# A threshold search with one number per row as its state, VectorE's keys in PSUM, and a one-hot made by one comparison

## The chip, the cores and the metric

One core of one Trainium2 chip runs the whole program in one launch. The metric is the device time in microseconds, median of the runs. The engines are TensorE (PE in the profile, PEld for its weight loads), VectorE (DVE), ScalarE (ACT), GpSimd (POOL) and SyncE (SP), which issues most DMA. SBUF is the on-chip memory, PSUM the accumulator memory that TensorE writes and that VectorE and ScalarE can read and write.

## The reference, cut to what matters

A layer takes 1024 tokens of width 1024 through a token mixer (gated DeltaNet and pooling) and then through a mixture of experts in which each of 16 experts chooses its 128 tokens:

```python
def expert_choice_ffn(h, w_router, w_gate, w_up, w_down):
    B_, L, D = h.shape
    cap = EC_CAPACITY * L // N_EXPERTS                       # 128
    aff = jax.nn.softmax((h @ w_router).astype(jnp.float32), axis=-1)
    top_aff, top_idx = lax.top_k(jnp.swapaxes(aff, 1, 2), cap)
    xe = jax.vmap(lambda hb, ib: hb[ib])(h, top_idx)
    hid = jax.nn.silu(jnp.einsum('becd,edf->becf', xe, w_gate)) * jnp.einsum('becd,edf->becf', xe, w_up)
    ye = jnp.einsum('becf,efd->becd', hid, w_down) * top_aff[..., None].astype(h.dtype)
    combine = lambda ib, yb: jnp.zeros((L, D), yb.dtype).at[ib.reshape(-1)].add(yb.reshape(-1, D))
    return jax.vmap(combine)(top_idx, ye)
```

The output is the final RMS-normalised stream of 1024 x 1024 numbers.

## The kernel before

The work runs in stages. After the token mixer comes the stage of its output projection and the router: it goes over 8 tiles of 128 tokens, and for each one multiplies by `w_out` (matmuls at L1256, into `y`), adds the residual, normalises, transposes and multiplies by the router's weights; `softmax` leaves the affinities in `aff`, 128 tokens x 8 tiles x 16 experts. The first tile of this stage is preceded by the constants of the later search, written by GpSimd (L1362 to L1393), and by `o_norm`, whose power at L1080 (`ro`) also runs on GpSimd; VectorE scales `oa` with it at L1082, and TensorE transposes that at L1105. Every engine executes its instructions in program order.

Then the search finds, for each of 16 experts, the affinity of its 128th best token. `aff` is transposed (L1534) so that each of 128 rows holds 128 affinities of one expert and one token tile; eight rows belong to one expert. The bits of an affinity are split into a high key (`khi`) and a low key (`klo`), and two searches of 7 and 8 rounds find the threshold, two bits in each round. A round compares all keys with three candidates: two on VectorE (L1562, `cmp`) and one on ScalarE with Sign (L1560), each with a sum along the row into `cnt`. A matmul with `same` (L1566) adds up the eight rows of an expert over a first matmul that puts the limits `lim` there (L1565), and VectorE counts from the totals how many candidates hold (L1579, `ge`, sum into `d`). The state of the search is the three candidates `nxt` and the last step `d`; two small instructions (L1568, L1569) make the next candidates and a third (L1558) the offset `c2` for ScalarE. During the first eight rounds ScalarE also rounds halves of the first four weight slices (L1574) and GpSimd subtracts (L1516, `flo`), and before that GpSimd finishes the FFN's input of the last two tiles (L1339, L1340) and stores it to `h2d`.

After the search, scans (L1602, L1603) give each chosen token its place, a transpose brings the places to token order (`tpp`, then `posT`), and `onehot(e)` compares them with the numbers 1 to 128: for expert 0 in one instruction on `tpp`, for the others in eight instructions, one for each token tile. `select` multiplies the one-hot with token numbers and affinities, and `gather` fetches the rows from `h2d` with an indirect DMA by GpSimd.

The expert stage goes over 16 experts with three weight matrices of 8 slices each (512 KB a slice). Each slice is loaded by SyncE's queue into one of 34 buffers, split into two parts (`fhi` on ScalarE, `flo` on VectorE at L1516) and used in six matmuls (L1638). A buffer is loaded again when its split is done. Results are added to `accd` by an indirect DMA (L1744). A last stage normalises and stores.

Of the kernel before, what the change touches and what calls it, by code (L numbers as in the profile page):

```python
# [19 lines left out]
L = 1024  # L20
NT = 8
# [5 lines left out]
CAP = 128  # L27
# [25 lines left out]
def trunk_kernel(ctx, tc, x, c, ctxt, c_ctx, w_mod, b_mod, norm1, norm2, w_in, conv_w, a_log, dt_bias,  # L53
# [154 lines left out]
    pos = [0]  # L208
# [1106 lines left out]
    def softmax(t):  # L1315
# [46 lines left out]
    SEARCH = [(65536.0, i) for i in range(7)] + [(1.0, i) for i in range(8)]  # L1362
    base3 = ES.tile([128, 3], F32, name="base3")
    sgn3 = ES.tile([128, 3], F32, name="sgn3")
    dlt3 = ES.tile([128, len(SEARCH), 3], F32, name="dlt3")
    stp3 = ES.tile([128, len(SEARCH), 3], F32, name="stp3")
    nxt0 = ES.tile([128, 2, 3], F32, name="nxt0")
    lim = ES.tile([128, 3], F32, name="lim")
    for j, v in enumerate((1.0, 2.0, -3.0)):
        POOL.memset(base3[:, j:j + 1], v)  # L1370
        POOL.memset(sgn3[:, j:j + 1], v / abs(v))
        POOL.memset(lim[:, j:j + 1], 0.5 - CAP if j < 2 else L - 2.0 * (CAP - 0.5))
    for n, (unit, i) in enumerate(SEARCH):
        POOL.memset(stp3[:, n, :], unit * 4.0 ** i)
        POOL.tensor_scalar(dlt3[:, n, :], base3, unit * ((4.0 ** (i - 1) if i else 0.0) - 4.0 ** i), None, op0=OP.mult)
    for n, (unit, i, first) in enumerate(((65536.0, 6, 0.0), (1.0, 7, 1.0))):
        POOL.tensor_scalar(nxt0[:, n, :], base3, unit * 4.0 ** i, None, op0=OP.mult)
        for j, v in enumerate((first, first, 0.5 * unit - first)):
            POOL.tensor_scalar(nxt0[:, n, j:j + 1], nxt0[:, n, j:j + 1], v, None, op0=OP.add)
# [12 lines left out]
    slotb = WS.tile([128, 128], BF16, name="slotb")  # L1392
    POOL.tensor_copy(slotb, slots)  # L1393
# [142 lines left out]
    khi = RT.tile([128, 128], F32, name="khi")  # L1536
    klo = RT.tile([128, 128], F32, name="klo")
    cmp = RT.tile([128, 2, 128], F32, name="cmp")
    ki = RT.tile([128, 128], I32, name="ki")
    DVE.tensor_scalar(ki, tpa.bitcast(I32), 0x7fff0000, None, op0=OP.bitwise_and)  # L1540
    DVE.tensor_copy(khi, ki)

    sgn = RT.tile([128, 128], F32, name="sgn")
    zero = RT.tile([128, 1], F32, name="zero")
    DVE.memset(zero, 0.0)
    thr = RT.tile([128, 2], F32, name="thr")

    def search(key, dst, nxt, unit, n):
# [3 lines left out]

        d = zero
        for i in range(n - 1, -1, -1):
            row = SEARCH.index((unit, i))
# [21 lines left out]
            ge = RT.tile([128, 3], F32, name="ge")  # L1577
            d = RT.tile([128, 1], F32, name="d", bufs=2)
# [3 lines left out]
    search(khi, thr[:, 0:1], nxt0[:, 0, :], 65536.0, 7)  # L1582
    ki = RT.tile([128, 128], I32, name="ki")
# [5 lines left out]
    search(klo, thr[:, 1:2], nxt0[:, 1, :], 1.0, 8)  # L1589
# [195 lines left out]
    pos = {}  # L1785
# [65 lines left out]
```

## Time and profile before

| | |
|---|---|
| median of 3 runs | 1363.76 us (1360.57 to 1364.97) |
| profiled execution, time | 1365.92 us |
| profiled execution, span | 1364.2 us |
| TensorE busy | 1261.2 us (92%) |
| VectorE busy | 1029.5 us (75%) |
| ScalarE busy | 751.1 us (55%) |
| GpSimd busy | 390.6 us (29%) |
| DMA, over the span | 241 GB/s |

The span goes from the first to the last instruction of the profiled execution; its time also holds what lies around them. Busy shares are means over stages with different limits, so a stage is read from its own stretch of the span. The granted clock of TensorE is given as a share of 2.4 GHz, and has the levels 1.00 and 0.50.

### The profile page before, as it was taken

The page shows a single profiled execution, that of the slowest core. Times are in us where ns is not written, and L with a number is a line of the kernel's source. Part 1 is how long each engine was busy: PE and PEld are TensorE (multiplying, and loading weights), DVE is VectorE, ACT ScalarE, POOL GpSimd, SP SyncE. Part 2 cuts the span into 40 slices and gives each one's busy share as a digit, 9 for nine tenths or more (in the row PEclk, how much of TensorE's full clock was granted, in tenths as well). Part 3 has the DMA queues.
Part 4 walks back from the last instruction along what each step waited for, and adds up shares of the span by engine and source line. Part 5 has one row for each costly group of instructions (what it writes and reads, how often), then busy time and mean ns, then how long its engine had stood idle before and what let it go on. Part 6 is the DMA issues. An engine that isn't in the chain of part 4 may idle for free.

```text
span 1364.2 us, 26631 instructions
## 1 busy us (share of the span) xinstructions
PE 1261.2 (92%) x10355; PEld 1003.4 (74%) x10355; DVE 1029.5 (75%) x1773; ACT 751.1 (55%) x1103; POOL 390.6 (29%) x394
## 2 busy tenths in 40 slices
PE   5899889989999989989982799999999999999997
PEld 3476777666767779978872688888888888888884
DVE  4763665675775436864659699999999999999995
ACT  5443434343433324333233477777777777777783
POOL 5700552494865113761116000000000000000002
PEclk9999989998999989999995799999999999999999
DMA  9667213212123268634686599999999999999806
GB/s 353 209 193 276 70 37 91 86 49 79 49 79 95 87 221 317 214 128 154 231 322 232 188 340 369 386 385 384 379 383 382 388 381 385 383 382 383 298 4 259
DMA packets 140760, 328.39 MB, mean 241 GB/s; under 512 B 13517, under 2 KB 53082, under 8 KB 140634
## 3 DMA queue, kind: packets, MB, share of 16 engines
q1 hardware_dynamic: 134826, 305.72, 60.8%
q0 software_dynamic: 5376, 19.40, 5.6%
q8 instruction: 81, 1.33, 0.4%
q10 hardware_dynamic: 432, 1.57, 0.3%
q14 instruction: 45, 0.37, 0.1%
HBM read 287.32 MB, written 39.32 MB: 239 GB/s over the span
## 4 chain that ended last, share of the span: by engine, by line
PE 75%; DVE 11%; issue 4%; POOL 4%; DMA 3%; ACT 2%; SPq 0%; POOLq 0%; ACTq 0%; DVEq 0%
PE pg L1638 14%; PE pu L1638 13%; PE pd L1638 12%; PE px L484 11%; PE y L1256 6%; PE sc L923 5%; PE iv L687 2%; DVE acc L428 2%; PE tp L1674 2%; PE gv L132 1%; DMA wm<-in_w_mod_dram 1%; DVE pT L666 1%; DMA Vd<-rows 1%; PE pc L484 1%; DVE T L704 1%
## 5 line engine op out<-in xcount | busy, mean ns | idle before, releaser
L484 PE MATMUL px<-hx,whi 128*128 128x512 f32 x640 | 222.0, 427 | 4.6 <-ACT hx L290 2.7
L1516 DVE TENSOR_TENSOR flo<-rawb,fhi 128x1024 fp32r<-128x1024 f32 x176 | 208.6, 1224 | 11.2 <-ACT fhi L1515 10.5
L1515 ACT ACTIVATE fhi<-rawb 128x1024 fp32r<-128x1024 f32 x176 | 186.1, 1062 | 53.6 <-PE pg L1638 19.0
L1516 DVE TENSOR_TENSOR flo<-rawa,fhi 128x1024 fp32r<-128x1024 f32 x158 | 187.3, 1224 | 12.9 <-ACT fhi L1515 12.2
L1515 ACT ACTIVATE fhi<-rawa 128x1024 fp32r<-128x1024 f32 x158 | 167.2, 1062 | 51.3 <-PE pg L1638 21.9
L1638 PE MATMUL pg<-fhi,lhs 128*128 128x512 f32 x544 | 157.9, 402 | 0.0
L1638 PE MATMUL pu<-fhi,lhs 128*128 128x512 f32 x512 | 146.6, 398 | 0.0
L484 PEld LDWEIGHTS px<-hx,whi 128*128 128x128 f32 x640 | 113.2, 193 | 40.5 <-issue 12.4
L1744 POOL DMA_INDIRECT accd<-ye,ix x15 | 34.6, 2310 | 366.2 <-DVE ye L1742 366.2
L1638 PE MATMUL pd<-fhi,lhs 128*128 128x512 f32 x480 | 134.2, 396 | 0.0
L484 PE MATMUL px<-hx,wlo 128*128 128x512 f32 x320 | 128.5, 402 | 0.0
L1638 PEld LDWEIGHTS pg<-fhi,lhs 128*128 128x128 f32 x544 | 100.8, 190 | 22.6 <-ACT lhs L1676 0.4
L1638 PEld LDWEIGHTS pu<-fhi,lhs 128*128 128x128 f32 x512 | 95.1, 188 | 21.8
L1638 PEld LDWEIGHTS pd<-fhi,lhs 128*128 128x128 f32 x480 | 90.1, 188 | 21.6
L1638 PE MATMUL pg<-flo,lhs 128*128 128x512 f32 x272 | 86.2, 398 | 0.0
L1638 PE MATMUL pu<-flo,lhs 128*128 128x512 f32 x256 | 80.5, 395 | 0.0
L1256 PE MATMUL y<-ohi,mx 128*128 128x512 f32 x256 | 76.4, 404 | 0.8 <-DVE oa L981 0.8
L201 POOL TENSOR_TENSOR wlo<-wraw,whi 128x1024 fp32r<-128x1024 f32 x16 | 41.1, 2568 | 125.2 <-ACT whi L200 125.2
L1638 PE MATMUL pd<-flo,lhs 128*128 128x512 f32 x240 | 75.5, 396 | 0.0
L484 PEld LDWEIGHTS px<-hx,wlo 128*128 128x128 f32 x320 | 61.6, 193 | 14.0
L428 DVE SCALAR_TENSOR_TENSOR acc<-pad,prmT,acc 128x1024 f32<-128x1024 f32 x36 | 66.3, 1843 | 3.6 <-ACT acc L424 3.3
L1664 POOL DMA_INDIRECT xe<-h2d,ix x16 | 16.4, 1027 | 168.7 <-PE pg L1638 120.7
(453 smaller groups left out, 2405.1 us busy)
## 6 DMA issues: line engine op xcount, KB each, us to landing
rawb<-in_w_down_dram SPq DMA_DIRECT2D x61, 512.0 KB, 6.1
rawb<-in_w_gate_dram SPq DMA_DIRECT2D x58, 512.0 KB, 5.1
rawb<-in_w_up_dram SPq DMA_DIRECT2D x57, 512.0 KB, 6.0
rawa<-in_w_gate_dram SPq DMA_DIRECT2D x56, 512.0 KB, 5.0
rawa<-in_w_up_dram SPq DMA_DIRECT2D x54, 512.0 KB, 6.1
rawa<-in_w_down_dram SPq DMA_DIRECT2D x52, 512.0 KB, 6.1
wm<-in_w_mod_dram SPq DMA_DIRECT2D x48, 512.0 KB, 5.7
wraw<-in_w_in_dram SPq DMA_DIRECT2D x20, 512.0 KB, 4.1
```

The lines of the kernel that those rows point to most:

```text
L201: (POOL if pos[0] > 4 else DVE).tensor_tensor(lo[:, :, :n], raw[:, :, :n], hi[:, :, :n].bitcast(F32), op=OP.subtract)
L428: DVE.scalar_tensor_tensor(acc, pad[:, j:j + L], convw(j, ct), acc, op0=OP.mult, op1=OP.add)
L484: PE.matmul(dst, wp[:, k, :], src[hp][:, k, o], start=start and i == 0, stop=stop and i == len(parts) - 1)
L687: PE.matmul(iv[r, u, o:64], pa[r, u, :], PV[r, u, o:64], start=True, stop=True)
L923: PE.matmul(p[:, h, :], lhs(h), rhs(h), start=True, stop=True)
L1256: PE.matmul(ys[t, hf][:, hf, :], l_[:, k, :], r_[:, 512 * hf:512 * hf + 512], start=(k == KORD[0] and i == 0), stop=(k == KORD[-1] and i = ...
L1515: ACT.activation(hi, raw, AF.Copy)
L1516: (eng or DVE).tensor_tensor(lo, raw, hi.bitcast(F32), op=OP.subtract)
L1638: PE.matmul(ps[:, hf, :], l_[:, k, :], r_[:, 512 * hf:512 * hf + 512], start=(k == 0 and n == 0), stop=(k == KD - 1 and n == 2))
L1664: POOL.indirect_dma_start(out=xe[e], out_offset=None, in_=h2d[:, :], in_offset=bass.IndirectOffsetOnAxis(ap=ix[:, 0:1], axis=0))
L1674: PE.transpose(tp[:, q, :], src[:, 128 * k:128 * k + 128], ident)
L1744: POOL.indirect_dma_start(out=accd[:, :], out_offset=bass.IndirectOffsetOnAxis(ap=idx.pop(e)[:, 0:1], axis=0), in_=ye, in_offset=None, com ...
```

## The change

The search's state becomes one number per row, the sum `v`, which `ge` accumulates straight into the constants' column of the next round: `stp5[:, row + 1, 3:4]`, beside a column of constants, which the two additional columns of `lim5` let pass. The candidates are `v` plus constants, so the instructions that made `c2` and `nxt` go. VectorE's keys lie in PSUM, and ScalarE has its own copy in SBUF (`keys`); the mask of integer bits `ki` is in PSUM too. The last tile's softmax leaves its exponentials in PSUM. `onehot` makes its mask by one comparison for every expert. The constants are made by other instructions on GpSimd.

```diff
@@ softmax
-        ACT.activation(a, a, AF.Exp, bias=mxn, accum_out=sm_)
+        ex = logits if t == ORDER[-1] else a
+        ACT.activation(ex, a, AF.Exp, bias=mxn, accum_out=sm_)
         DVE.reciprocal(rc, sm_)
-        DVE.tensor_scalar(a, a, rc, None, op0=OP.mult)
+        DVE.tensor_scalar(a, ex, rc, None, op0=OP.mult)
@@ constants
-    for j, v in enumerate((1.0, 2.0, -3.0)):
-        POOL.memset(base3[:, j:j + 1], v)
-        POOL.memset(sgn3[:, j:j + 1], v / abs(v))
-        POOL.memset(lim[:, j:j + 1], 0.5 - CAP if j < 2 else L - 2.0 * (CAP - 0.5))
+    SEARCH = [(65536.0, i) for i in range(6, -1, -1)] + [(1.0, i) for i in range(7, -1, -1)]
+    cst3 = ES.tile([128, len(SEARCH), 2], F32, name="cst3")
+    stp5 = ES.tile([128, len(SEARCH) + 1, 5], F32, name="stp5")
+    lim5 = ES.tile([128, 5], F32, name="lim5")
+    for j, v in enumerate((0.5 - CAP, 0.5 - CAP, L - 2.0 * (CAP - 0.5), 1.0, 1.0)):
+        POOL.memset(lim5[:, j:j + 1], v)
     for n, (unit, i) in enumerate(SEARCH):
-        POOL.memset(stp3[:, n, :], unit * 4.0 ** i)
-        POOL.tensor_scalar(dlt3[:, n, :], base3, unit * ((4.0 ** (i - 1) if i else 0.0) - 4.0 ** i), None, op0=OP.mult)
-    for n, (unit, i, first) in enumerate(((65536.0, 6, 0.0), (1.0, 7, 1.0))):
-        POOL.tensor_scalar(nxt0[:, n, :], base3, unit * 4.0 ** i, None, op0=OP.mult)
-        for j, v in enumerate((first, first, 0.5 * unit - first)):
-            POOL.tensor_scalar(nxt0[:, n, j:j + 1], nxt0[:, n, j:j + 1], v, None, op0=OP.add)
+        step = unit * 4.0 ** i
+        third = 3.0 * step - 0.5 * unit
+        for j in range(2):
+            POOL.memset(cst3[:, n, j:j + 1], (j + 1) * step - third)
+        POOL.memset(stp5[:, n, 0:3], -step)
+        if n in (0, 7):
+            POOL.memset(stp5[:, n, 3:4], -third - (1.0 if n else 0.0))
+        POOL.memset(stp5[:, n, 4:5], third - (0.75 * step - 0.5 * unit if i else 0.0))
...
-    slotb = WS.tile([128, 128], BF16, name="slotb")
-    POOL.tensor_copy(slotb, slots)
@@ search
-    khi = RT.tile([128, 128], F32, name="khi")
-    klo = RT.tile([128, 128], F32, name="klo")
+    khi = PSR.tile([128, 128], F32, name="khi")
+    klo = PSR.tile([128, 128], F32, name="klo")
+    keys = RT.tile([128, 2, 128], F32, name="keys")
-    ki = RT.tile([128, 128], I32, name="ki")
+    ki = PSR.tile([128, 128], I32, name="ki")
     DVE.tensor_scalar(ki, tpa.bitcast(I32), 0x7fff0000, None, op0=OP.bitwise_and)
+    DVE.tensor_copy(keys[:, 0, :], ki)
     DVE.tensor_copy(khi, ki)
...
+        for row in rows:
+            v = stp5[:, row, 3:4]
             cnt = RT.tile([128, 3], BF16, name="cnt", bufs=8)
-            c2 = RT.tile([128, 1], F32, name="c2", bufs=15)
-            DVE.tensor_tensor(c2, nxt[:, 2:3], d, op=OP.subtract)
-                ACT.activation(sgn, key, AF.Sign, bias=c2, accum_out=cnt[:, 2:3])
+                ACT.activation(sgn, skey, AF.Sign, bias=v, accum_out=cnt[:, 2:3])
             for j in range(2):
-                DVE.scalar_tensor_tensor(cmp[:, j, :], key, d, nxt[:, j:j + 1].to_broadcast([128, 128]),
-                                         op0=OP.subtract, op1=OP.is_ge, accum_out=cnt[:, j:j + 1])
-            tot = PSR.tile([128, 3], F32, name="tot", bufs=2)
-            PE.matmul(tot, ident, lim, start=True, stop=False)
-            PE.matmul(tot, same, cnt, start=False, stop=True)
-            new = RT.tile([128, 3], F32, name="nxt", bufs=8)
-            DVE.scalar_tensor_tensor(new, sgn3, d, nxt, op0=OP.mult, op1=OP.add)
-            DVE.tensor_tensor(new, new, dlt3[:, row, :], op=OP.add)
-            nxt = new
+                DVE.scalar_tensor_tensor(cmp[:, j, :], key, v, cst3[:, row, j:j + 1].to_broadcast([128, 128]),
+                                         op0=OP.add, op1=OP.is_ge, accum_out=cnt[:, j:j + 1])
+            tot = PSR.tile([128, 5], F32, name="tot", bufs=2)
+            PE.matmul(tot, ident, lim5, start=True, stop=False)
+            PE.matmul(tot[:, 0:3], same, cnt, start=False, stop=True)
...
-            DVE.scalar_tensor_tensor(ge, tot, 0.0, stp3[:, row, :], op0=OP.is_ge, op1=OP.mult, accum_out=d)
-        DVE.tensor_tensor(dst, nxt[:, 0:1], d, op=OP.add)
+            DVE.scalar_tensor_tensor(ge, tot, 0.0, stp5[:, row, :], op0=OP.is_ge, op1=OP.mult,
+                                     accum_out=dst if row == rows[-1] else stp5[:, row + 1, 3:4])
+        DVE.tensor_scalar(dst, dst, -1.0, None, op0=OP.mult)
@@ between the searches
+    kl = RT.tile([128, 128], F32, name="kl")
     DVE.tensor_scalar(ki, tpa.bitcast(I32), 0xffff, None, op0=OP.bitwise_and)
-    DVE.tensor_scalar(klo, ki, 1.0, None, op0=OP.add)
-    DVE.scalar_tensor_tensor(klo, khi, thr[:, 0:1], klo, op0=OP.is_equal, op1=OP.mult)
+    DVE.tensor_scalar(kl, ki, 1.0, None, op0=OP.add)
+    DVE.scalar_tensor_tensor(kl, khi, thr[:, 0:1], kl, op0=OP.is_equal, op1=OP.mult)
     DVE.tensor_scalar(khi, khi, thr[:, 0:1], 1.0e6, op0=OP.is_gt, op1=OP.mult)
-    DVE.tensor_tensor(klo, klo, khi, op=OP.add)
+    DVE.tensor_tensor(keys[:, 1, :], khi, kl, op=OP.add)
+    DVE.tensor_tensor(klo, khi, kl, op=OP.add)
@@ onehot
-        if pos is not None:
-            DVE.tensor_tensor(oh, slots[:, None, :].to_broadcast([128, NT, 128]),
-                              pos[:, :, e:e + 1].to_broadcast([128, NT, 128]), op=OP.is_equal)
-        else:
-            for t in range(NT):
-                DVE.tensor_scalar(oh[:, t, :], slotb, posT[:, t, e:e + 1], None, op0=OP.is_equal)
+        DVE.tensor_tensor(oh, slots[:, None, :].to_broadcast([128, NT, 128]),
+                          (posT if pos is None else pos)[:, :, e:e + 1].to_broadcast([128, NT, 128]), op=OP.is_equal)
```

## Rows read from the trace of the kernel before

**Rows 1.** Windows of four stages: stretch, its length, busy times, clock, DMA share, GB/s.

```profile
600.00:620.00 20.00, 16.12 (x76) 13.36 (x75) 7.27 (x14) 5.00 (x9) 8.65 (x36) 0.83 0.51 187
...
660.00:680.00 20.00, 20.00 (x128) 15.99 (x127) 12.07 (x22) 6.40 (x15) 3.62 (x6) 1.00 0.63 216
...
740.00:760.00 20.00, 6.79 (x42) 5.65 (x42) 16.10 (x92) 3.94 (x16) 3.43 (x2) 0.50 0.13 36
...
840.00:1240.00 400.00, 400.00 (x1884) 323.73 (x1883) 386.29 (x470) 315.79 (x326) 36.72 (x22) 1.00 1.02 384
```

**Rows 2.** Timeline, 594 to 612 us: start, duration, engine, line, operation, shapes [idle before].

```profile
594.43 0.10 POOL L1370 MEMSET base<- 128x1 f32 x1
...
594.46 0.10 POOL L1371 MEMSET sgn<- 128x1 f32 x1
...
600.95 0.16 DVE L1079 SCALAR_TENSOR_TENSOR ro<-ro,ssqh 128x4 f32<-128x4 f32 x1
...
604.53 0.14 POOL L1384 IOTA jt<- 128x8 f32 x1
...
606.06 1.05 POOL L1080 TENSOR_TENSOR ro<-ro,mhalf 128x4 f32<-128x4 f32 x1
...
607.89 1.12 PE L1105 MATMUL tp<-ident,oa 128*128 128x128 f32 x4 [3.88 <-DVE oa L1082]
```

**Rows 3.** Timeline around the start of the search, 713 to 722 us.

```profile
714.06 1.36 DVE L1328 TENSOR_SCALAR aff<-aff,sm 128x16 f32<-128x16 f32 x1
...
716.05 0.29 DVE L1540 TENSOR_SCALAR ki<-tp 128x128 int32<-128x128 int32 x1 [0.63 <-PE tp L1534]
...
716.37 1.52 DVE L1541 CAST khi<-ki 128x128 f32<-128x128 int32 x1
...
718.01 0.34 DVE L1562 SCALAR_TENSOR_TENSOR cmp<-khi,zero,nxt 128x128 f32<-128x128 f32 x1
...
721.22 2.35 POOL L1340 TENSOR_TENSOR h<-h,s2b 128x1024 f32<-128x1024 f32 x1
...
721.28 0.15 DVE L1579 SCALAR_TENSOR_TENSOR ge<-tot,stp 128x3 f32<-128x3 f32 x1
...
721.48 2.11 DVE L1558 TENSOR_TENSOR c<-nxt,d 128x1 f32<-128x1 f32 x1
```

**Rows 4.** Timeline of one round of the second search, 744 to 746 us.

```profile
744.54 0.16 DVE L1579 SCALAR_TENSOR_TENSOR ge<-tot,stp 128x3 f32<-128x3 f32 x1
...
744.74 0.16 DVE L1558 TENSOR_TENSOR c<-nxt,d 128x1 f32<-128x1 f32 x1
...
744.82 0.34 DVE L1562 SCALAR_TENSOR_TENSOR cmp<-klo,d,nxt 128x128 f32<-128x128 f32 x1
...
745.02 0.40 ACT L1560 ACTIVATE sgn<-klo,c 128x128 f32<-128x128 f32 x1 [0.73 <-PE tot L1565]
...
745.36 0.09 DVE L1562 DVE_READ_ACCUMULATOR cmp<-klo,d,nxt 128x1 bf16 x1
...
745.57 0.17 PE L1566 MATMUL tot<-cnt,same 128*128 128x3 bf16 x1 [0.64 <-ACT sgn L1560]
...
745.77 0.16 DVE L1579 SCALAR_TENSOR_TENSOR ge<-tot,stp 128x3 f32<-128x3 f32 x1
```

**Rows 5.** Timeline, weight splits on GpSimd, then the way to the first expert.

```profile
728.29 4.64 POOL L1516 TENSOR_TENSOR flo<-rawa,fhi 128x1024 fp32r<-128x1024 f32 x2
...
751.74 0.42 DVE L1602 TENSOR_TENSOR_SCAN cmp<-onesr,ar 128x128 f32<-128x128 f32 x1
...
756.34 1.39 DVE L1621 TENSOR_SCALAR oh<-slotb,posT 128x128 bf16<-128x128 bf16 x8
...
761.58 1.76 PE L1674 MATMUL tp<-ident,xe 128*128 128x128 f32 x7 [3.60 <-DMA xe<-h2d,ix]
```

**Rows 6.** The page's costliest groups: busy, mean ns | idle before, its releaser.

```profile
L1516 DVE TENSOR_TENSOR flo<-rawb,fhi 128x1024 fp32r<-128x1024 f32 x176 | 208.6, 1224 | 11.2 <-ACT fhi L1515 10.5
...
L1744 POOL DMA_INDIRECT accd<-ye,ix x15 | 34.6, 2310 | 366.2 <-DVE ye L1742 366.2
```

More of the change, by code (lines that the diff above doesn't have):

```diff
@@ L1358, in trunk_kernel @@
     DVE.tensor_tensor(prev, d16, same, op=OP.mult)
[L1362 to L1368, printed above, removed]
-    for j, v in enumerate((1.0, 2.0, -3.0)):
-        POOL.memset(base3[:, j:j + 1], v)
-        POOL.memset(sgn3[:, j:j + 1], v / abs(v))
-        POOL.memset(lim[:, j:j + 1], 0.5 - CAP if j < 2 else L - 2.0 * (CAP - 0.5))
-    for n, (unit, i) in enumerate(SEARCH):
-        POOL.memset(stp3[:, n, :], unit * 4.0 ** i)
-        POOL.tensor_scalar(dlt3[:, n, :], base3, unit * ((4.0 ** (i - 1) if i else 0.0) - 4.0 ** i), None, op0=OP.mult)
-    for n, (unit, i, first) in enumerate(((65536.0, 6, 0.0), (1.0, 7, 1.0))):
-        POOL.tensor_scalar(nxt0[:, n, :], base3, unit * 4.0 ** i, None, op0=OP.mult)
-        for j, v in enumerate((first, first, 0.5 * unit - first)):
-            POOL.tensor_scalar(nxt0[:, n, j:j + 1], nxt0[:, n, j:j + 1], v, None, op0=OP.add)
+    SEARCH = [(65536.0, i) for i in range(6, -1, -1)] + [(1.0, i) for i in range(7, -1, -1)]
[4 more added lines that the diff above has]
+        POOL.memset(lim5[:, j:j + 1], v)
+    for n, (unit, i) in enumerate(SEARCH):
+        step = unit * 4.0 ** i
[6 more added lines that the diff above has]
+        POOL.memset(stp5[:, n, 4:5], third - (0.75 * step - 0.5 * unit if i else 0.0))
     vals = WS.tile([128, NX, NT, 5], BF16, name="vals")
@@ L1541, in trunk_kernel, with search @@
     DVE.tensor_copy(khi, ki)
     sgn = RT.tile([128, 128], F32, name="sgn")
-    zero = RT.tile([128, 1], F32, name="zero")
-    DVE.memset(zero, 0.0)
     thr = RT.tile([128, 2], F32, name="thr")
[L1548 to L1555, printed above, removed]
+    def search(key, skey, dst, rows):
+        for row in rows:
+            v = stp5[:, row, 3:4]
             cnt = RT.tile([128, 3], BF16, name="cnt", bufs=8)
-            c2 = RT.tile([128, 1], F32, name="c2", bufs=15)
-            DVE.tensor_tensor(c2, nxt[:, 2:3], d, op=OP.subtract)
@@ L1576, in search @@
                     split_slice(POOL)
-            ge = RT.tile([128, 3], F32, name="ge")
-            d = RT.tile([128, 1], F32, name="d", bufs=2)
-            DVE.scalar_tensor_tensor(ge, tot, 0.0, stp3[:, row, :], op0=OP.is_ge, op1=OP.mult, accum_out=d)
-        DVE.tensor_tensor(dst, nxt[:, 0:1], d, op=OP.add)
-    search(khi, thr[:, 0:1], nxt0[:, 0, :], 65536.0, 7)
-    ki = RT.tile([128, 128], I32, name="ki")
+            ge = RT.tile([128, 5], F32, name="ge")
+            DVE.scalar_tensor_tensor(ge, tot, 0.0, stp5[:, row, :], op0=OP.is_ge, op1=OP.mult,
+                                     accum_out=dst if row == rows[-1] else stp5[:, row + 1, 3:4])
+        DVE.tensor_scalar(dst, dst, -1.0, None, op0=OP.mult)
+    search(khi, keys[:, 0, :], thr[:, 0:1], range(7))
+    kl = RT.tile([128, 128], F32, name="kl")
     DVE.tensor_scalar(ki, tpa.bitcast(I32), 0xffff, None, op0=OP.bitwise_and)
-    DVE.tensor_scalar(klo, ki, 1.0, None, op0=OP.add)
-    DVE.scalar_tensor_tensor(klo, khi, thr[:, 0:1], klo, op0=OP.is_equal, op1=OP.mult)
+    DVE.tensor_scalar(kl, ki, 1.0, None, op0=OP.add)
+    DVE.scalar_tensor_tensor(kl, khi, thr[:, 0:1], kl, op0=OP.is_equal, op1=OP.mult)
     DVE.tensor_scalar(khi, khi, thr[:, 0:1], 1.0e6, op0=OP.is_gt, op1=OP.mult)
-    DVE.tensor_tensor(klo, klo, khi, op=OP.add)
-    search(klo, thr[:, 1:2], nxt0[:, 1, :], 1.0, 8)
+    DVE.tensor_tensor(keys[:, 1, :], khi, kl, op=OP.add)
+    DVE.tensor_tensor(klo, khi, kl, op=OP.add)
+    search(klo, keys[:, 1, :], thr[:, 1:2], range(7, 15))
     nge = RT.tile([128, 2], BF16, name="nge")
```

## The prediction

> **What bounds the kernel now.** I read the windows first, since the kernel is a row of stages with different limits [rows 1]. In the expert stage, from 780 us on, TensorE is a solid block of matmuls (400.00 of 400 us from 840 to 1240), with VectorE close behind (386.29). Nothing in there gets shorter by this change, so the question is when the block starts. Before it lie two places where TensorE stands still. One is the search (720 to 760; the window from 740 shows 6.79 busy, clock 0.50, DMA 36 GB/s: the weight buffers are full and everybody waits for VectorE). The other is seen only in the clock column: 600 to 620 has 16.12 busy and a mean clock of 0.83.
>
> Then the timeline around 600 [rows 2]. TensorE waits 3.88 us at L1105 for VectorE's `oa`, which waits for GpSimd's power `ro` (L1080). Its input is ready at 600.95 + 0.16 = 601.11, but GpSimd takes it up at 606.06, because it is still writing the search's constants, which it began at 594.43. So the constants are on the path.
>
> Then the timeline of the search [rows 3]. While GpSimd runs a tensor operation, some VectorE instructions stretch to its end: `c` on one element takes 2.11, the cast to `khi` 1.52, the softmax's last product 1.36. Others run through untouched in the same time: `ge` reads PSUM and one SBUF tensor and takes 0.15 at 721.28, inside GpSimd's operation of 721.22; `ki`, which reads PSUM, takes 0.29 at 716.05. What stretches has two SBUF tensors, or copies SBUF to SBUF. Six instructions of the rounds stretch like this one, about 2.1 us each, 12.8 in all.
>
> Last, one round with GpSimd idle [rows 4], ge to ge 1.23: ge, `c`, then on ScalarE Sign (0.28 after `c` starts), 0.55 to the matmul, 0.20 to the next ge.
>
> **The change, part by part.**
>
> *Constants.* Removed are 47 GpSimd instructions, 24 of them memsets; added are 67 memsets (5 + 15 x 4 + 2). Memsets follow each other at 0.03 us (594.43, 594.46) and last 0.10 [rows 2], so 67 cost 2.2 to 6.7 us, ending at 596.7 to 601.1. What stays behind them, from `jt` to the power, took 604.53 to 606.06, 1.5 (the copy `slotb` in it also goes; not counted). The power starts at the later of 601.2 (its input) and 598.2 to 602.6, and TensorE gets its operand 1.83 later (606.06 to 607.89): 603.0 to 604.4. TensorE is free at 607.89 - 3.88 = 604.01. So the idle time goes, or shrinks to 0.4. The clock should then not fall: a mean of 0.83 over 20 us is 6.8 us at 0.50 [rows 1], the lower of the two levels (1.2 GHz), and it follows this idle time; some 6.2 us of that is work (607.89 on), which takes 3.1 less at 2.4 GHz. I take 2.7, since at full speed the third transpose there will wait a little for its PSUM buffer. Stage gain 3.9 + 2.7 = 6.6; bounds 0 and 7.0. After it TensorE has no gap up to 710 (660 to 680 shows 20.00 [rows 1]), so the gain is carried on.
>
> *Start of the search.* The last softmax's product and the copies out of `ki` now read PSUM: 1.36 to about 0.24 and 1.52 to about 0.29, less one added copy of 0.27: 2.1 earlier, first comparison at 718.01 - 2.1 = 715.9 (times from here on are on the old time line).
>
> *Rounds.* Without `c`, `nxt` and `dlt` the loop has two paths [rows 4]. By ScalarE: 0.28 (ge to Sign, `c` taken out) + 0.55 + 0.20 = 1.03. By VectorE: 0.20 (ge to comparison) + 0.54 (two comparisons, to the read of the accumulator) + at most 0.21 to the matmul + 0.20 = 1.15. I take 1.10. No row has a 128x128 comparison reading PSUM; the bounds are 1.03 (as from SBUF) and 1.35 (each comparison 0.1 dearer and more). None of the rounds' instructions keeps two SBUF tensors, so the six stretches (12.8) go; bounds all of them or none.
>
> *Between and after the rounds.* From 718.01 to the scan at 751.74 [rows 5] is 33.73; less a first round of 0.95, 14 x 1.23 = 17.2 and the 12.8, 2.8 remain for the step between the two searches and the end. One more addition and the sign flips make it 3.1. So the scan could start at 715.9 + 0.9 + 14 x 1.10 + 3.1 = 735.3, 16.4 earlier.
>
> *What is late next.* GpSimd's four weight splits. The first two run back to back from 728.29 [rows 5], 2.32 each; they wait for GpSimd's earlier work, which the change leaves as it is. ScalarE's halves, one a round, now come earlier, so all four run without a break: until 728.29 + 4 x 2.32 = 737.57. The scans (L1602, L1603) and `rk`, `rq` have two SBUF tensors each. The scan is therefore held from 735.3 to 737.57. No row has a scan beside GpSimd; the nearest are the stretched `c` and its like, so I let it wait. From the scan to the first transposes of gathered rows took 751.74 to 761.58, 9.84, and is kept. Stage gain 751.74 - 737.57 = 14.2; bounds 13.0 (rounds of 1.35) and 16.4 (no waiting). The splits also cap what a dearer comparison can cost: up to 1.25 a round it is hidden.
>
> The Trainium skill, page "SBUF — State Buffer", section "Who interferes with whom", says that a VectorE instruction with two SBUF inputs is blocked by a GpSimd instruction that reads SBUF, and that with one SBUF input outside the two-port modes it is not. By that the scan is held and the gain is 14.2; if scans were exempt it would be 16.4. The rows of `c` and ge agree with it.
>
> *One-hot.* Eight compares (1.39 together [rows 5]) become one over 1024 elements; a two-input operation of that size takes 1.22 [rows 6]. Costed at nothing: TensorE's solid block covers it, and VectorE has 3.4% to spare there. Without that cover it would be -0.2 per expert.
>
> *Weights.* DMA stands almost still (36 GB/s in 740 to 760): the buffers are full before the search ends, and will be at 747 too. Later loads are released by VectorE's splits, so they move with the block.
>
> **Sum.** The profiled execution has a span of 1364.2 and a time of 1365.92. 1365.92 - 6.6 - 14.2 = 1345.1. It lies 2.2 above the median of the runs (1363.76), so on their scale 1343.0.
>
> **Rivals.**
> 1. The splits don't hold the scan: gain 16.4 + 6.6 = 23.0, 1340.8. For it: an instruction can slip in between two splits; against: the next one meets the next split. 0.12.
> 2. The idle time goes, the clock falls all the same, or a rest of the gap stays: 3.9 + 14.2 = 18.1, 1345.7. 0.15.
> 3. The constants stay on the path, since 67 memsets in a row cost GpSimd more than the 0.10 of a single one: from 0.15 each nothing is left of the 6.6. Gain 14.2, 1349.6. Against it: nine in a row took 0.3. 0.10.
> 4. The change does not do what it says: comparisons out of PSUM are stretched like those out of SBUF. Then only 15 x 0.13 less the added copy, 1.5, and the 6.6 remain: 1355.7. Against it stands ge at 721.28. 0.06.
> 5. Slower: the one-hot now reads two SBUF tensors, and waits for GpSimd's two descriptor jobs of an expert, a scatter's preparation being 2.31 [rows 6], 4.6 for both. Over 14 experts that is 14 x (4.6 - 0.2) = 62, of which VectorE's spare 3.4% of some 550 us takes up 19; the other 43 make it 1363.8 - 20.8 + 43 = 1386. It decides from 3.0 of stretch per expert on ((20.8 + 19) / 14 + 0.2). Against it: 176 splits on VectorE, with two SBUF tensors each, ran at a mean of 1224 beside those very jobs [rows 6]. 0.03. The same section of the Trainium skill's page speaks for it, in that a two-SBUF-input instruction contends with GpSimd's reads; the splits' row shows nothing of that for descriptor jobs.
> 6. Gain and loss about cancel: for instance weights arrive too late for the earlier start. 0.04.
>
> **From this the numbers.** The forecast (gain 19 to 22, own range 1341.5 to 1345) has 0.50. The range takes in rivals 1 to 3: 1339 to 1351, some 0.85. A measurement of this kernel tells no change from 0.3%, 4.1 us. Faster: the forecast and rivals 1 to 4, 0.93; same: rival 6, 0.04; slower: rival 5, 0.03.
>
> **What would show it.** In the new profile: (a) no wait of TensorE at L1105, and the clock at 1.00 through 608 to 614; (b) comparisons all alike, none above 0.5 us, and rounds of 1.0 to 1.2; (c) GpSimd's four splits without a gap, the scan stretched to the end of the last; (d) the gather some 21 us earlier by the clock of the span, and the expert block of the same length. It is wrong if TensorE still waits at L1105, if rounds are above 1.35, or if gaps appear in the expert block.

## The result, and the profile after

The changed kernel takes 1343.20 us in the median of 4 runs (1340.47 to 1344.65); the kernel before, run beside it, takes 1362.45 (1360.57 to 1364.97, 4 runs). The ratio is 0.9855, with a 95% interval of 0.983 to 0.988: 19.25 us less. The forecast was 1343.0. Every experiment below has its ratio to the kernel before run beside it (medians 1361.86 to 1363.85), so the ratios are to be compared, and the stages of the profiles, more than the medians.

The profiled execution of the changed kernel has a time of 1344.65 us, a span of 1342.9 and a mean granted clock of 0.974 (before: 1365.92, 1364.2, 0.960). All rows of this section are of this execution. First the windows, with the columns of [rows 1].

```profile
600.00:620.00 20.00, 18.35 (x104) 15.23 (x103) 10.40 (x19) 6.63 (x12) 4.14 (x6) 1.00 0.61 211
660.00:680.00 20.00, 20.00 (x108) 16.14 (x107) 13.94 (x25) 5.65 (x13) 1.81 (x3) 1.00 0.79 269
740.00:760.00 20.00, 19.00 (x75) 15.23 (x76) 12.32 (x11) 12.70 (x13) 0.97 (x1) 0.85 0.72 246
840.00:1240.00 400.00, 400.00 (x1895) 323.91 (x1895) 385.58 (x396) 315.73 (x326) 43.00 (x23) 1.00 1.02 384
```

In 600 to 620 the clock is 1.00 instead of 0.83, and TensorE has 18.35 of work instead of 16.12. In 740 to 760, where it stood still before, it is in the expert block. The block itself is as solid as it was.

The timeline of the stage at 600, which answers to [rows 2]:

```profile
593.01 2.44 DVE L1356 TENSOR_SCALAR pmod<-jp 128x128 int32<-128x128 int32 x1 [0.20 <-POOL jp L1351]
...
593.20 0.10 POOL L1378 MEMSET stp<- 128x1 f32 x1
593.24 0.10 POOL L1379 MEMSET stp<- 128x1 f32 x1
...
595.18 0.10 POOL L1379 MEMSET stp<- 128x1 f32 x1
...
601.77 0.16 DVE L1079 SCALAR_TENSOR_TENSOR ro<-ro,ssqh 128x4 f32<-128x4 f32 x1
602.01 1.03 POOL L1080 TENSOR_TENSOR ro<-ro,mhalf 128x4 f32<-128x4 f32 x1 [5.38 <-DVE ro L1079]
...
603.82 0.66 PE L1105 MATMUL tp<-ident,oa 128*128 128x128 f32 x4 [1.30 <-DVE oa L1082]
...
605.26 0.65 PE L1069 MATMUL tp<-ident,A 128*128 128x128 f32 x4 [0.35 <-DVE fpt L1108]
```

GpSimd is free long before the power's input comes, and takes it up at once (602.01). But TensorE still waits 1.30 at L1105, because that input is late: VectorE's `pmod` took 2.44 us beside GpSimd's 67 memsets, which ran from 592.93 to 595.28. So the constants are off GpSimd's path and have moved onto VectorE's. The prediction had named a wait at L1105 as a sign of being wrong, and here it is.

The same stretch of the kernel before has something that the prediction did not read:

```profile
594.51 0.40 DVE L1355 TENSOR_SCALAR pmod<-jp 128x128 int32<-128x128 int32 x1 [0.20 <-POOL jp L1350]
...
595.69 4.62 DVE L1057 TENSOR_TENSOR olo<-oraw,ohi 128x1024 fp32r<-128x1024 f32 x4
...
597.00 1.13 POOL L1375 TENSOR_SCALAR dlt<-base 128x3 f32<-128x3 f32 x1
...
600.51 0.23 POOL L1375 TENSOR_SCALAR dlt<-base 128x3 f32<-128x3 f32 x1
```

While VectorE ran four subtractions with two SBUF inputs (`olo`, until 600.31), four of GpSimd's tensor_scalars took 1.03 to 1.13 each; the eight like them from 600.51 on took 0.23, and the memsets between them 0.10 throughout. That is some 3.4 of the 4.95 us that GpSimd came late to the power (601.11 to 606.06). By these rows VectorE held GpSimd here, as GpSimd holds VectorE elsewhere; no experiment takes the subtractions away to show it.

The timeline at the start of the search ([rows 3]) and of one round of the first search ([rows 4]):

```profile
707.56 0.23 DVE L1329 TENSOR_SCALAR aff<-lg,sm 128x16 f32<-128x16 f32 x1
...
708.61 0.29 DVE L1541 CAST keys<-ki 128x128 f32<-128x128 int32 x1
708.82 0.29 DVE L1542 CAST khi<-ki 128x128 f32<-128x128 int32 x1
708.91 2.35 POOL L1341 TENSOR_TENSOR h<-h,s2b 128x1024 f32<-128x1024 f32 x1
...
709.14 0.35 DVE L1557 SCALAR_TENSOR_TENSOR cmp<-khi,stp,cst 128x128 f32<-128x128 f32 x1
...
711.18 0.17 DVE L1569 SCALAR_TENSOR_TENSOR ge<-tot,stp 128x5 f32<-128x5 f32 x1 [0.28 <-PE tot L1561]
...
711.38 0.35 DVE L1557 SCALAR_TENSOR_TENSOR cmp<-khi,stp,cst 128x128 f32<-128x128 f32 x1
711.45 0.40 ACT L1555 ACTIVATE sgn<-keys,stp 128x128 f32<-128x128 f32 x1
...
711.66 0.35 DVE L1557 SCALAR_TENSOR_TENSOR cmp<-khi,stp,cst 128x128 f32<-128x128 f32 x1
...
712.08 0.19 PE L1561 MATMUL tot<-cnt,same 128*128 128x3 bf16 x1 [0.50 <-DVE cmp L1557]
```

Nothing is stretched, although GpSimd's sums run until 711.26 and again from 712.24: the softmax's product takes 0.23 instead of 1.36, and no comparison of the search, the rounds beside the later splits included, takes more than 0.35. The counting instruction comes again at 712.30, so a round is 1.12; in the second search the seven distances are 1.18 to 1.19.

The end of the search ([rows 5]):

```profile
721.46 9.24 POOL L1514 TENSOR_TENSOR flo<-rawa,fhi 128x1024 fp32r<-128x1024 f32 x4
...
729.19 1.80 DVE L1594 TENSOR_TENSOR_SCAN cmp<-onesr,ar 128x128 f32<-128x128 f32 x1
730.91 0.39 DVE L1595 TENSOR_TENSOR_SCAN cmp<-onesr,eq 128x128 f32<-128x128 f32 x1
...
735.17 1.22 DVE L1608 TENSOR_TENSOR oh<-slots,posT 128x1024 bf16<-128x1024 f32 x1
...
736.00 1.33 POOL L1652 DMA_INDIRECT xe<-h2d,ix  x1 [5.29 <-issue]
...
741.00 1.97 PE L1662 MATMUL tp<-ident,xe 128*128 128x128 f32 x8 [4.18 <-DMA xe<-h2d,ix]
```

The four splits run without a gap until 730.70, and the first scan, ready at 729.19, is held until 730.99.

For the experiments I cut the span at four marks: the first output matmul of the stage (L1256, `y`); GpSimd's input sum of the last tile but one (L1339, here L1340: at 713.05 before and 706.49 here; the expectations call it the last input sum); the first transposes of gathered rows; and the start of VectorE's last instruction.

| kernel | first output matmul at | to the input sum | to the gathered rows | to the last instruction |
|---|---|---|---|---|
| before | 594.06 | 118.99 | 48.53 | 596.98 |
| before, second profile | 592.80 | 117.62 | 48.63 | 596.16 |
| changed | 592.55 | 113.94 | 34.51 | 596.32 |
| changed, second profile | 591.30 | 113.94 | 34.51 | 596.19 |

So the search gives 14.0 us, the stage at 600 gives 5.1 against one profile of before and 3.7 against the other, and the block gives 0.7 against the one and nothing against the other. The first column is code that the change doesn't touch; 1.5 of the 21.3 us between the profiled executions (1365.92 and 1344.65) lies there.

### The profile page after: what moved, and what is told of

It is laid out like the page before. It is cut to its first block, busy times and chain, and to the rows that moved or that the text cites. A ratio compares the mean times of both kernels' runs of the same rounds, so it can differ in the third digit from the quotient of the medians.

```text
span 1342.9 us, 26508 instructions
## 1 busy us (share of the span) xinstructions
PE 1253.6 (93%) x10355; PEld 995.8 (74%) x10355; DVE 1012.2 (75%) x1624; ACT 750.1 (56%) x1103; POOL 386.7 (29%) x413
## 3 DMA queue, kind: packets, MB, share of 16 engines
q8 instruction: 81, 1.33, 0.4%
## 4 chain that ended last, share of the span: by engine, by line
PE 77%; DVE 10%; issue 3%; POOL 3%; DMA 3%; ACT 2%; SPq 0%; POOLq 0%; ACTq 0%; DVEq 0%
PE pg L1626 14%; PE pu L1626 13%; PE pd L1626 13%; PE px L484 12%; PE y L1256 6%; PE sc L923 5%; PE iv L687 2%; DVE acc L428 2%; PE tp L1662 2%; DMA wm<-in_w_mod_dram 1%; PE gv L132 1%; PE pc L484 1%; DVE pT L666 1%; DVE T L704 1%; DVE cmp L1557 1%
## 5 line engine op out<-in xcount | busy, mean ns | idle before, releaser
L1256 PE MATMUL y<-ohi,mx 128*128 128x512 f32 x256 | 75.5, 400 | 0.8 <-DVE oa L981 0.8
L1652 POOL DMA_INDIRECT xe<-h2d,ix x16 | 22.9, 1433 | 159.3 <-PE pg L1626 120.7
```

Of the source, the lines that this page charges most:

```text
L1256: PE.matmul(ys[t, hf][:, hf, :], l_[:, k, :], r_[:, 512 * hf:512 * hf + 512], start=(k == KORD[0] and i == 0), stop=(k == KORD[-1] and i = ...
L1652: POOL.indirect_dma_start(out=xe[e], out_offset=None, in_=h2d[:, :], in_offset=bass.IndirectOffsetOnAxis(ap=ix[:, 0:1], axis=0))
```

## The experiments

**The constants.** The kernel before, with its constants written by memsets and nothing else changed:

```diff
-        POOL.tensor_scalar(dlt3[:, n, :], base3, unit * (...), None, op0=OP.mult)
+        for j, v in enumerate((1.0, 2.0, -3.0)):
+            POOL.memset(dlt3[:, n, j:j + 1], v * unit * (...))
... (nxt0 likewise; base3 goes)
```

> The kernel before with its own constants made by 72 memsets in place of memsets and tensor_scalars; the search as before. Theory (the constants were on TensorE's path): TensorE's wait at L1105 falls from 3.9 to 1.0 to 1.6 us and the clock stays at 1.00 in 600 to 620, 5 us faster than before, 1357 to 1358; VectorE's pmod is held to the end of the memsets (2.4 us or more), which is why the wait does not vanish. Rival (GpSimd's other work holds the power anyway, or the clock falls at any wait): under 2 us faster.

Measured: 1361.48 us (10 runs), ratio 0.9985 (0.997 to 0.9999). TensorE's wait at L1105 is 1.55 instead of 3.88, and tile 0's first output matmul to tile 1's takes 17.41 instead of 22.24 (595.98 to 613.39). The stage behaves as the theory has it; the median, where 5 us were expected, shows under 1 us of it, as the rival had it. I ran the same kernel again, and both kernels unchanged for second profiles.

> The kernel before with its constants written by memsets, a second time, because the median of the first time (0.8 us less than before) did not show what its stage at 600 had gained (tile 0's first output matmul to tile 1's: 17.41 instead of 22.24). Theory (the stages ahead of it, whose code is the same, start it at a time that varies from run to run by some us): the stage takes 17.4 (+-0.3) again, from its first output matmul to the end of the span it is 764.7 to 765.5 instead of 770.1, and the median is 3 to 6 us less than that of before. Rival (where the constants are written in this way, the stages ahead or the search give the gain back): the stage's first matmul lies at 595.5 or later again, and the median is 0 to 2 us less.

> The kernel before once more, for a second profile of it. Theory: from the first output matmul to the end of the span 770.1 (+-0.7), while that matmul lies anywhere from 589 to 597. Rival (the stages ahead take a time that is the kernel's own): 594.1 (+-0.3).

> The changed kernel once more, for a second profile of it. Theory: from the first output matmul to the end of the span 750.35 (+-0.5) again, while that matmul itself may lie anywhere from 589 to 597; the stage takes 17.2 with a wait of 1.3 and the first scan about 1.8. Rival (the wait of 1.3, or the scan's stretch, is itself a chance of that one profile): it is missing or twice as long, and 750.35 changes by more than 1.

Measured: 1361.46 (12 runs) against 1363.85, ratio 0.9989 (0.9971 to 1.0008), and the changed kernel 1344.50 (5 runs), ratio 0.9871 (0.9847 to 0.9895). The stage took 18.99 this time, not 17.4; in the kernel before it took 20.86 (592.80 to 613.66), not 22.24; in the changed kernel 17.18 both times. From the first output matmul to the end of the span the memset kernel took 766.8, above the expected 764.7 to 765.5, and its median missed the expected 3 to 6 us too; the changed kernel took 750.30, with a wait of 1.31 and a scan of 1.82, as expected. The window 600 to 620 tells why. First the memset kernel's first profile, then its second, then the second of before:

```profile
600.00:620.00 20.00, 18.10 (x99) 14.96 (x98) 12.27 (x20) 4.88 (x9) 4.50 (x8) 1.00 0.62 214
```
```profile
600.00:620.00 20.00, 18.11 (x92) 14.86 (x91) 10.76 (x17) 4.88 (x9) 3.12 (x5) 0.91 0.63 214
```
```profile
600.00:620.00 20.00, 16.16 (x84) 13.48 (x83) 6.53 (x12) 4.99 (x9) 7.47 (x30) 0.91 0.45 170
```

With the same wait (1.55 and 1.54) the clock held once and fell once, for some 0.09 x 20 x 2 = 3.6 us at 0.50; before, it fell for 6.8 us in one profile [rows 1] and 3.6 in the other. The mean stage is 21.55 before and 18.20 with memsets, 3.35 less, which lies inside both intervals of the memset kernel (up to 4.1 and 4.0 us). The first output matmul lay at 595.98 and 594.40, so the rival, that it comes later in this kernel, has the first profile for it and not the second; over all 14 profiles of this study it lies from 589.47 to 596.49 with no order by kernel. The second profile of before also missed its own expectation: from that matmul to the end of the span it took 768.0, not 770.1, for the same reason, the clock.

The changed kernel with its memsets moved behind the memset of `wrm`, which GpSimd does after the power:

```diff
             POOL.memset(big["wrm"], 0.0)
+            for j, v in enumerate((0.5 - CAP, ...)):
+                POOL.memset(lim5[:, j:j + 1], v)
+            for n, (unit, i) in enumerate(SEARCH): ...
             y_mm(t[0], KORD[7:])
```

> The changed kernel with the 67 memsets moved behind the first power and the memset of wrm in GpSimd's order. Theory (the row of memsets held VectorE's pmod, and that held the power): pmod 0.4 us, no wait at L1105 above 0.2 us, 1.0 to 1.5 us faster than the changed kernel, some 1342. Rival (the two casts to vals or the splits on VectorE hold the power): the wait at L1105 stays at 1 us or more, no gain.

Measured: 1343.81 us (4 runs), ratio 0.9859 (0.9838 to 0.988). From its timeline:

```profile
592.87 0.23 DVE L1356 TENSOR_SCALAR pmod<-jp 128x128 int32<-128x128 int32 x1 [0.20 <-POOL jp L1351]
...
599.60 1.02 POOL L1080 TENSOR_TENSOR ro<-ro,mhalf 128x4 f32<-128x4 f32 x1 [5.37 <-DVE ro L1079]
...
602.19 0.60 PE L1105 MATMUL tp<-ident,oa 128*128 128x128 f32 x4
```

`pmod` takes 0.23, the power starts 7.20 us after the stage's first matmul (592.40) instead of 9.46, the wait at L1105 is gone, and the stage takes 15.64 instead of 17.18. That settles who was late: `pmod`, held by the row of memsets. The expected 1342 did not come out of the median, which can't show 1.5 us among runs that spread over some 4.

**The keys and the state, each alone.** The changed kernel with VectorE's keys and `ki` in SBUF, one copy for both engines:

```diff
-    khi = PSR.tile([128, 128], F32, name="khi")
-    klo = PSR.tile([128, 128], F32, name="klo")
-    keys = RT.tile([128, 2, 128], F32, name="keys")
+    khi = RT.tile([128, 128], F32, name="khi")
+    klo = RT.tile([128, 128], F32, name="klo")
...
-    ki = PSR.tile([128, 128], I32, name="ki")
+    ki = RT.tile([128, 128], I32, name="ki")
...
```

> The changed kernel with khi, klo and ki in SBUF again, one copy for both engines; everything else as changed. Theory (keys in PSUM free the comparisons from GpSimd): the comparisons have two SBUF tensors again and stretch to the end of GpSimd's operation; with five to seven such stretches of some 2.1 us the scan starts 9 to 13 us later than in the changed kernel, time 1352 to 1356, while TensorE's start at 600 keeps its gain. Rival (the shorter loop alone gave the gain): no comparison above 0.5 us, time within 2 us of 1343.

The kernel before with only its keys (and `ki`) moved to PSUM, and a copy in SBUF for ScalarE:

```diff
-    khi = RT.tile([128, 128], F32, name="khi")
-    klo = RT.tile([128, 128], F32, name="klo")
+    khi = PSR.tile([128, 128], F32, name="khi")
+    klo = PSR.tile([128, 128], F32, name="klo")
+    keys = RT.tile([128, 2, 128], F32, name="keys")
...
```

> The kernel before with only the keys moved to PSUM (and ScalarE's copy in SBUF); candidates nxt, d and c2 as before. Theory: comparisons no longer stretch, but c2, nxt and its second instruction still have two SBUF tensors and stretch instead, so that at least four stretches of about 2 us stay: 1357 to 1362, 0 to 5 us faster than before. Rival (the place of the keys is all that matters): at least 10 us faster than before.

Measured: 1358.11 us (10 runs), ratio 0.9975 (0.9958 to 0.9991), for the first; 1361.87 (10 runs), 0.9998 (0.9982 to 1.0015), for the second. From the input sum to the gathered rows they take 47.39 and 47.66, against 48.53 before and 34.51 with both. So each half by itself gives about 1 us of the 14. (The first also keeps the new constants; to the input sum it takes 113.93, as the changed kernel does, so what its median gains lies mostly there.) Timelines, first of the one with its keys in SBUF, then of the one with the old state:

```profile
709.09 2.57 DVE L1555 SCALAR_TENSOR_TENSOR cmp<-khi,stp,cst 128x128 f32<-128x128 f32 x1
709.15 2.35 POOL L1340 TENSOR_TENSOR h<-h,A2b 128x1024 f32<-128x1024 f32 x1
...
711.58 2.34 POOL L1341 TENSOR_TENSOR h<-h,s2b 128x1024 f32<-128x1024 f32 x1
...
711.59 2.47 DVE L1555 SCALAR_TENSOR_TENSOR cmp<-khi,stp,cst 128x128 f32<-128x128 f32 x1
```
```profile
724.67 0.35 DVE L1564 SCALAR_TENSOR_TENSOR cmp<-khi,d,nxt 128x128 f32<-128x128 f32 x1
724.69 4.63 POOL L1516 TENSOR_TENSOR flo<-rawa,fhi 128x1024 fp32r<-128x1024 f32 x2
...
724.94 2.11 DVE L1570 SCALAR_TENSOR_TENSOR nxt<-sgn,d,nxt 128x3 f32<-128x3 f32 x1
...
727.08 2.26 DVE L1571 TENSOR_TENSOR nxt<-nxt,dlt 128x3 f32<-128x3 f32 x1
```

In the first the comparisons are stretched, in the second the comparisons run through and the instructions on three elements wait in their place. Added up over the rounds (each duration less the shortest of its like, where that is over 0.1) it is 14.6 in the first and 13.2 in the second, and 13.0 before by the same count, where the prediction had 12.8. The stall comes with GpSimd's work, and falls on whichever instruction with two SBUF tensors comes next; only when none is left in the rounds does it go. The second kernel kept its comparisons clean, so its expectation held; the first was right in kind, but its scan starts 14.0 later than in the changed kernel instead of 9 to 13, and its median is some 2 us above the upper end that I gave.

The second kernel's stage at 600 has the constants of before and is a third sample of it: TensorE's wait is 3.83, the clock in 600 to 620 is 0.83 again, and the stage takes 21.97; to the input sum it is 118.73, 4.8 more than in the changed kernel.

**What sets a round.** The changed kernel with the first comparison of each round made twice:

```diff
-            for j in range(2):
+            for j in (0, 0, 1):
```

> The changed kernel with the first of the two comparisons of each round made twice (its second result replaces the first). Theory (a round is set by VectorE's two comparisons, not by ScalarE's Sign, and GpSimd's splits cover a part of what a dearer round costs): each of 15 rounds takes 0.27 more, 1.39 instead of 1.12, so the scan could start 4.1 later; 1.4 of that lies under the stretch in which the scan was held, and from GpSimd's last input sum to the first transposes of gathered rows it takes 37.2 instead of 34.5. The time is 2.7 more than the changed kernel's. Rival A (ScalarE's path sets the round): 1.12 to 1.2, 34.5. Rival B (all of it on the path): 38.6.

Measured: 1349.36 us (4 runs), ratio 0.991 (0.988 to 0.994), 4.9 more than the changed kernel on the same chip. Its timeline of one round:

```profile
710.75 0.17 DVE L1569 SCALAR_TENSOR_TENSOR ge<-tot,stp 128x5 f32<-128x5 f32 x1 [0.28 <-PE tot L1561]
...
710.96 0.35 DVE L1557 SCALAR_TENSOR_TENSOR cmp<-khi,stp,cst 128x128 f32<-128x128 f32 x1
...
711.36 0.35 DVE L1557 SCALAR_TENSOR_TENSOR cmp<-khi,stp,cst 128x128 f32<-128x128 f32 x1
711.63 0.09 DVE L1557 DVE_READ_ACCUMULATOR cmp<-khi,stp,cst 128x1 bf16 x1
711.63 0.35 DVE L1557 SCALAR_TENSOR_TENSOR cmp<-khi,stp,cst 128x128 f32<-128x128 f32 x1
```

The round is 1.52 (710.75 to 712.27), not 1.39: a comparison that writes the same tile and the same count as the one ahead of it starts 0.40 after it, where one that writes others starts 0.27 after. VectorE sets the round (rival A falls). The scan is ready 6.07 later (28.77 after the input sum instead of 22.70) and takes 0.42 again; the gathered rows come only 4.57 later (39.08), so 1.5 is hidden by the splits, near the 1.4 expected (rival B falls, at 0.40 a comparison it would be 40.6).

**What holds the scan.** The changed kernel with the two 0/1 tiles that scans and places read in PSUM:

```diff
-    gt = RT.tile([128, 128], F32, name="ar")
-    eq = RT.tile([128, 128], F32, name="eq")
+    gteq = PSR.tile([128, 2, 128], F32, name="gteq")
+    gt, eq = gteq[:, 0, :], gteq[:, 1, :]
```

> The changed kernel with the two 0/1 tiles that the scans and the two place instructions read in PSUM, so that none of these four keeps two SBUF tensors. In the changed kernel the first scan began at 729.19 and took 1.80 instead of 0.42, until 0.29 after the end of GpSimd's row of splits (730.70). Theory (the scan is held as an instruction with two SBUF inputs): it now takes 0.4 to 0.5 while the splits still run, and the time from the start of the scan to the first transposes of gathered rows falls from 11.81 to 10.4. Rival (a scan waits for GpSimd wherever its data lie, or a scan out of PSUM is itself dearer): 1.8 again, 11.8. The whole: 1.4 us less by the theory, 0 by the rival, both less than the 4.1 us that a measurement tells, so the trace decides.

Measured: 1345.06 us (4 runs), ratio 0.9871 (0.9843 to 0.9898). From the timeline:

```profile
725.25 9.25 POOL L1514 TENSOR_TENSOR flo<-rawa,fhi 128x1024 fp32r<-128x1024 f32 x4
...
733.47 0.42 DVE L1594 TENSOR_TENSOR_SCAN cmp<-onesr,gteq 128x128 f32<-128x128 f32 x1
733.81 0.40 DVE L1595 TENSOR_TENSOR_SCAN cmp<-onesr,gteq 128x128 f32<-128x128 f32 x1
```

The scan takes 0.42 while the splits run until 734.50, and from its start to the gathered rows it is 10.30. From the first of the two instructions that write the 0/1 tiles to the scan it takes 0.98 instead of 0.55 with the tiles in PSUM, so 1.04 is left from the input sum on (33.47).

The same with late memsets, a candidate for the best version:

> The changed kernel with the memsets of the search's constants placed behind the memset of the router's buffer in GpSimd's order, and the scan's 0/1 tiles in PSUM. Theory: both gains stand side by side, since one lies in the stage at 600 (tile 0's first output matmul to tile 1's: 17.18 to 15.6) and the other behind the search (scan to first transposes 11.81 to 10.4): 2.9 us less than the changed kernel, about 1340.3. Rival (the expert block can't start earlier, because the gather or the weights hold it): 1343.2 again, and a gap of TensorE ahead of the first transposes that is longer by what was gained.

Measured: 1344.75 us (6 runs, 1338.91 to 1345.86), ratio 0.9864 (0.9842 to 0.9887). In its profile both gains stand (stage 15.63, input sum to gathered rows 33.49), and from the first output matmul to the end of the span it takes 747.6 instead of 750.35. But that matmul lay at 596.49, and the median shows none of it: neither variant can be told from the changed kernel by it.

The changed kernel with the last softmax's exponentials in SBUF (`ex = a`):

> The changed kernel with the last tile's exponentials back in SBUF. Theory (an instruction from SBUF to SBUF on VectorE is held by GpSimd, and the splits set the time of the scan): the last product of the softmax takes 1.2 to 1.4 instead of 0.23, the first comparison comes about 1.1 later (3.75 after the start of GpSimd's last input sum, instead of 2.65), and nothing of it is left at the end, since the scan is held until the end of the splits anyway: its row shrinks from 1.80 to about 0.7, and from GpSimd's last input sum to the first transposes of gathered rows it stays 34.5 (+-0.3). Rival (all of VectorE's time ahead of the scan is on the path): 35.6. The whole time 0 or 1.1 more, not to be told by the median.

Measured: 1342.53 us (one run). Its timeline:

```profile
705.35 1.35 DVE L1329 TENSOR_SCALAR aff<-aff,sm 128x16 f32<-128x16 f32 x1
...
728.24 0.57 DVE L1594 TENSOR_TENSOR_SCAN cmp<-onesr,ar 128x128 f32<-128x128 f32 x1
```

The product is stretched to 1.35, the first comparison comes 1.2 later (3.87 after the input sum, instead of 2.65), the scan's hold shrinks to 0.15, and the gathered rows come at 34.42, as without the edit. So the PSUM exponentials, one of the parts of the change, bring nothing in this profile: the scan is held until the splits end.

**The one-hot.** The changed kernel with the eight compares for each expert but the first:

```diff
...
+            for t in range(NT):
+                DVE.tensor_scalar(oh[:, t, :], slotb, posT[:, t, e:e + 1], None, op0=OP.is_equal)
```

> The changed kernel with the eight compares per expert of before instead of one comparison with two SBUF inputs (expert 0 keeps its own). Theory (the one-hot costs nothing, covered by TensorE's solid block): the time from the first transposes of gathered rows to the end of the last expert's matmuls stays within 0.7 of 574.57, VectorE is busier by 0.2 an expert, and the median stays within 1.5 of 1343.2. In front of the block, GpSimd's job for the first gather falls from 1.33 back to 1.09, if it was the one-hot's two SBUF inputs beside it that made it longer, and from the second scan to the first transposes it takes 9.5 to 9.8 instead of 10.09. Rival (the one comparison waits for GpSimd's descriptor jobs in every expert): the block gets shorter by 14 times what such a wait takes, 2 us or more.

Measured: 1345.89 us (4 runs), ratio 0.9879 (0.9853 to 0.9905). From the gathered rows to the end of the last expert's matmuls it takes 574.75 (574.57 expected), to the last instruction 596.52 (596.32 in the changed kernel). VectorE is busy for 386.33 of the 400 us from 840 to 1240, instead of 385.58, which is less than the 0.2 an expert that I expected. The median came out 2.7 above 1343.2, more than the 1.5 expected, but the intervals of the two ratios overlap, and in the profile the first output matmul lies 2.8 later than the changed kernel's (595.39), in code that is the same. GpSimd's first gather:

```profile
738.08 1.39 DVE L1615 TENSOR_SCALAR oh<-slotb,posT 128x128 bf16<-128x128 bf16 x8
738.91 1.09 POOL L1658 DMA_INDIRECT xe<-h2d,ix  x1 [5.29 <-issue]
```

It takes 1.09 as before, not 1.33, and second scan to gathered rows is 9.69 instead of 10.09. The six profiles with eight compares agree (job 1.07 to 1.10, second scan to gathered rows 9.49 to 9.85), and so do the eight with one comparison (1.33 to 1.34, 9.87 to 10.39). The form of the one-hot costs 0.4 once, and nothing that shows in the block.

## Why the prediction was right, and where it was not

*The search* was right in mechanism and size: 14.2 forecast, 14.0 measured (48.53 to 34.51). Its steps, on the old time line (6.56 added): first comparison at 715.9, measured 715.70; scan ready at 735.3, measured 735.75, since rounds are 1.12 and 1.19 instead of 1.10; splits' end 737.57, measured 737.26; gathered rows at 747.4, measured 747.56. The last two agree by two small errors that offset each other: the splits end 0.31 earlier, and from there it takes 10.30 instead of the 9.84 that was kept, mostly because the one-hot was costed at nothing and costs 0.4 ahead of the first gathered rows. No comparison out of PSUM is slowed (0.35): rival 4 falls. The splits hold the scan: rival 1 falls, and the scan with one SBUF tensor, which ran through the same splits in 0.42, shows that it was the two SBUF tensors. The rule that was cited there, of the Trainium skill, page "SBUF — State Buffer", section "Who interferes with whom", agrees with the scan (1.80 beside the splits, 0.42 with one input in PSUM), with the comparisons (2.57 and 0.35) and with the operations on three elements (2.11, and 0.21 without GpSimd) alike.

*The stage at 600* is the term that was mis-sized: 6.6 forecast, 5.1 against the profile shown, 3.7 and 4.8 against the two others of the old constants. The step that failed is "the power starts at the later of 601.2 (its input)": that input was taken from the profile of before, as if the memsets touched GpSimd's own queue alone. They held `pmod` on VectorE, the input came at 601.93, which is 603.44 on the old line, and TensorE still waited 1.30 at L1105, the prediction's own sign of being wrong. With the memsets elsewhere the step holds (power 2.26 earlier in the stage, no wait). The same section of the Trainium skill's page says that `tensor_scalar` can enter a mode that takes both of VectorE's port pairs, and that in such a mode it contends with GpSimd; its limit to GpSimd operations that read stands with two SBUF inputs only. The 2.44 beside memsets, which read nothing, and the 0.23 without them fit that, though no run here shows which mode `pmod` ran in, and the prediction had used only the section's other rule. The clock part (2.7) was right for the profile shown: of the 5.1, 2.6 are idle time and 2.5 the clock; of the 3.7, 2.5 and 1.1. Of rival 2 the rest of the gap came true (1.30), the fall of the clock did not: in all nine profiles of the changed kernel and its variants, with waits of 1.28 to 1.72 or none, it held at 1.00 from 592 to 620. That was not sure beforehand, as the memset kernel shows, whose clock fell after 1.54.

*The sum.* 20.8 was forecast and 19.25 measured, 1.55 less. That the time of 1343.0 came within 0.2 of 1343.20 is luck: the kernel before came out 1.3 lower beside it (1362.45) than the median that the sum started from. The gather, forecast some 21 us earlier, is 21.2 earlier (757.17 to 736.00), but 1.5 of that is the earlier start of the stage, in untouched code.

*The rest.* The one-hot costs nothing in the block (rival 5 falls). The weights were there in time, since the block is no longer than before (596.32 and 596.98; rival 6 falls). The constants left GpSimd's path (rival 3 falls: memsets in a row cost 0.034 each).

What stays open: the memset constants alone moved the median by 0.8 and 2.4 us, where their stage moved by 3.35 in the mean of two profiles. The intervals allow both. In the three profiles with a wait of 3.8 us the clock fell each time, in the nine with 1.28 to 1.72 once: too few to say how often it falls.

## What to carry to other kernels

While GpSimd works, look for every VectorE instruction that keeps two tensors in SBUF, however small, in a loop that others wait for: moving one operand of some of them to PSUM only hands the wait to the next, and the gain comes with the last of them. Look the other way too: an engine that is late may itself have been held, as GpSimd's constants seem to have been beside VectorE's subtractions. When work is moved off one engine's queue, look also at what runs beside it on the other of these two engines, not only at what is queued behind it. Cut the span at marks and compare stages: here untouched code moved by 7 us from run to run, and edits worth 1.5 us were plain in their stage and invisible in the median.

## What the runs showed of the hardware that was not expected

- A row of 67 short memsets held a VectorE instruction like one long operation: 2.44 us in place of 0.23, until about the end of the row, though each memset took 0.10 (starts 0.03 to 0.04 apart). Before, the row that `pmod` met was ten memsets long and ended at 594.83; `pmod` took 0.40, to 594.91.
- Four GpSimd tensor_scalars on three elements took 1.03 to 1.13 each beside VectorE's subtractions, and 0.23 without them; memsets beside the same subtractions took 0.10. All three profiles with the old constants show it.
- TensorE's clock fell after a wait of 1.54 us in one execution and held after 1.55 in another of the same kernel, and after 1.72 in the kernel with three comparisons; in the kernel before, after 3.88 and 3.84, it stayed at 0.50 for 6.8 us once and for 3.6 once.
- An accumulating comparison into the tile and count that the previous one wrote started 0.40 after it, into others 0.27 after; which of the two makes the difference was not tested.
- GpSimd's job for a gather took 1.33 beside the one-hot of 1024 elements, and 1.09 beside eight compares of 128.
